# A two-layer diffusion trunk: the slot table written behind the routing and read in the second expert, one modulation bank computed during the routing

## The chip, the core and the metric

The kernel runs on one NeuronCore of a Trainium2 chip. The metric is the device time of one execution in microseconds; the median of three runs stands for the kernel. Engines: PE (TensorE) multiplies matrices, DVE (VectorE) and ACT (ScalarE) do elementwise work, POOL (GpSimd) issues indirect transfers, SP issues most weight loads. The DMA engines move all data; an issuing engine only starts a transfer.

## The reference

Two layers over 256 context and 256 latent tokens of width 1024. Each layer starts from modulation vectors, six per stream, that come from the conditioning alone:

```python
mod_x = split(silu_c @ w_ada + b_ada, 6)        # latents; the same with silu_cc for the context
h  = rms_norm(x, norm1) * (1 + mod[1]) + mod[0]
px = h @ w_in                                   # retention, convolution and latent attention in parallel
x_mid = x + mod[2] * merge_branches(...)
h2 = rms_norm(x_mid, norm2) * (1 + mod[4]) + mod[3]
x  = x_mid + mod[5] * moe(h2)                   # 16 experts in 4 groups, each token goes to 2 experts
```

`moe` scores each token with a shared router, chooses the best group and two experts in it, and adds `gate * (silu(h2 @ w1[e]) * (h2 @ w3[e])) @ w2[e]` over the chosen experts. All is float32. In layer 0 both streams (512 tokens) go through `moe`, in layer 1 the latents only.

## The kernel before

**Precision.** Every float32 weight is split into a high half (`ehi`, a cast on ACT, L1018) and a low half (`elo`, a subtraction on DVE, L1020); a product is three matmuls: high by high and high by low, then low by high (`mm6`, L192 to L195).

**Modulation banks.** `w_ada` of a layer is cut into three banks of 2048 columns. `Ada(l, b)` computes one: eight steps of one 128-row block, each with four matmuls on four column groups of PE (eight in the trace, L274), then a bias add (L278, L281) and four small stores to `modd[l]` (`finish`). `prep` clears and loads the bias rows on POOL (L246 to L256). Bank (0, 0) comes first; the other five, bank (1, 2) last of them, are filled into layer 0's mixing, one step behind each projection (`fill`). Bank (1, 2) holds the vectors 4 and 5 of layer 1, first read far into layer 1. Its blocks come as 1 MB loads into one buffer, `adaw`.

**Routing of layer 0.** Behind the output projection, the logits of four token tiles are computed (L1109); small DVE operations choose the experts (`select`) and number the tokens of each expert (`positions`: two matmuls, L1279 and L1280). An expert takes at most 112 tokens. For experts 0 and 1, `fetch(e, True)` compares slot numbers and finds the token indices with one-hot matmuls (L1591, L1592), casts them (`si`, L1593) and gathers the rows from `h2d` by an indirect transfer on POOL (L1598). For the other experts the indices come from a table: `slot_table` scatters token number and gate of each token's two choices into DRAM (eight indirect transfers, L1568), loads the eight parts back (`tabs`, L1572), adds them up on DVE (L1573) and makes the indices `sis` (L1574).

**Expert loop.** An expert has two projections up (`up`, four quarters each, each quarter one 512 KB piece of `w1` or `w3`), `act`, and the projection down (`finish`, four quarters). In iteration `e` the order is: first `up` of `e`, with the turning of `e - 1`'s hidden rows ahead of its second quarter; down of `e - 1`; second `up` of `e`; `act`; turning of the rows of `e + 1` (`turn_x`, L1609); `fetch(e + 2)`. In iteration 0 the slot table is built behind the first `up`. Weight pieces are loaded in the order of the list `pieces` into 25 buffers; the use of a piece frees its buffer, and `prefetch` then issues the next load on SP. A callable in `later` runs at the next quarter (`follow`).

**Order.** The program's text gives priorities; the framework's scheduler orders each engine's instructions by them and by when it expects an operand, and each engine then runs its instructions strictly in that order. `tc.issue_after(ins)` (`queued`) puts instructions behind another one of their engine.

Of the kernel before, what the change touches and what calls it, by code (L numbers as in the profile page):

```python
# [108 lines left out]
def tile_hybrid(ctx, tc, x, c, ctxt, c_ctx, w_ada, b_ada, norm1, norm2, w_in, ret_decay, ret_gn, w_ret_o,  # L109
# [123 lines left out]
    class Ada:  # L233
# [30 lines left out]
        def step(self, k):  # L264
            l, b = self.l, self.b
            if k == 5:
                self.prep()
            if k == 0:
                self.ps = psa.tile([P, 512], F32, name=nm("psa"), tag="psa")
            if k not in self.w:  # L270
                self.load(k)
            w = self.w.pop(k)
            for g in range(4):
                TE.matmul(self.ps[32 * g:32 * g + 32, :], sC[:, k, :], w[:, g * 512:(g + 1) * 512],  # L274
                          start=(k == 0), stop=(k == KD - 1))
            if k == KD - 1:
                m = self.bias[0]
                V.tensor_tensor(m, self.ps, m, op=ALU.add)  # L278
                if b != 1:
                    q = slice(64, 128) if b == 0 else slice(0, 64)  # L280
                    V.scalar_tensor_tensor(m[q, :], m[q, :], 1.0, self.bias[1][q, :], op0=ALU.add, op1=ALU.mult)  # L281

# [44 lines left out]
    for l in range(DEPTH):  # L327
# [95 lines left out]
        if l == 0:  # L423
# [74 lines left out]
            ma = stA.enter_context(pool(f"mb{l}", side="right"))  # L498
            for al, ab_ in ((0, 1), (0, 2), (1, 0), (1, 1), (1, 2)):
                a = Ada(al, ab_, mx, 1, ps_tile, t2)  # L500
                todo += [(a, k) for k in range(KD + 1)]
# [467 lines left out]
        NA, NB = (7, 6) if l == 0 else (5, 6)  # L969
        pieces = []  # L970
        for e in range(NE):
# [33 lines left out]
        def queued(ins):  # L1005
            return tc.issue_after(ins) if ins is not None else nullcontext()

        def weights(after=(None, None)):

# [12 lines left out]
            prefetch()  # L1022
            return [t.rearrange("p (k n) -> p k n", k=kt) for t in (hi, lo)]


# [81 lines left out]
        def logits_part(t, half):  # L1107
            for k in range(4 * half, 4 * half + 4):
                TE.matmul(lps[0][:, t * NE:(t + 1) * NE], hTs[t, half][:, k % 4 * P:(k % 4 + 1) * P],  # L1109
                          wrs[(T0 + t) // 2][:, k, :], start=(k == 0), stop=(k == KD - 1))  # L1110

# [103 lines left out]
        if l == 0:  # L1215
            offer(3, lambda: wr_.tile([P, 1024], F32, name=nm("wraw"), tag="wraw", bufs=NRAW), REST[l])
            prefetch()
        lps[0] = ps_tile()
        for t in range(NTT):
            ps = ps_tile()  # L1220
            for k in range(KD):
# [7 lines left out]
                if t and k == 5:  # L1229
# [3 lines left out]
                    if t - 1 == 1:  # L1233

                        for tg in ("mr20", "mr40", "mr30"):
                            offer(1, lambda tg=tg: me.tile([P, 1024], F32, name=nm("eraw"), tag=tg), 1000 if tg == "mr30" else REST[l])
                        prefetch()
# [60 lines left out]
        for i in range(4):  # L1298
            offer(1, lambda i=i: zz[:, i, :], FOR[l])
        if l == 0:  # L1300
            offer(ND[l], lambda: et("eraw3", [P, 1024], F32, ND[l]))
            offer(1, lambda: et("fx", [P, 1024]), REST[l])
            prefetch(most=6)
            with queued(h2w[-1]):
                prefetch(nc.gpsimd, 2)
        else:
            offer(1, lambda: me.tile([P, 1024], F32, name=nm("eraw"), tag="mr21"), REST[l])
            prefetch()
# [222 lines left out]
        if l == 0:  # L1531
# [21 lines left out]
            def slot_table():  # L1553
# [19 lines left out]
                V.tensor_reduce(gtab.rearrange("p e v -> p (e v)"), tabs.rearrange("p j n -> p n j"), axis=AX.X, op=ALU.add)  # L1573
                V.tensor_scalar(sis, gtab[:, :, 1], 1.0, 0.0, op0=ALU.subtract, op1=ALU.max)  # L1574

# [8 lines left out]
            def fetch(e, early=False):  # L1584

                if early:
                    si = et("si", [P, 1], I32, 2)
                    ip = ps_tile()
                    for t in range(NTT):
                        oh16 = et("oh16", [P, cap], F16, 4)  # L1590
                        V.tensor_scalar(oh16, C("iota")[:, :cap], posm[:, t, e:e + 1], None, op0=ALU.is_equal)  # L1591
                        TE.matmul(ip[:cap, 0:1], oh16, tok16[:, t:t + 1], start=(t == 0), stop=(t == NTT - 1))  # L1592
                    routed.append(V.tensor_copy(si[:cap, :], ip[:cap, 0:1]).ins)  # L1593
# [59 lines left out]
            def collect(t):  # L1653
# [11 lines left out]
            with tc.issue_after(fetch(1, True)):  # L1665
                prefetch(nc.gpsimd)
            turn_x(0)
            th = None
            for e in range(NE):
# [29 lines left out]
                if e == 0:  # L1699
                    offer(1, lambda: mg.tile([P, 1024], F32, name=nm("eraw"), tag="xe2"), REST[l])  # L1700
# [209 lines left out]
```

## Time and profile before

| | |
|---|---|
| runs | 1657.21 us median (1655.49 to 1659.54) |
| the profiled execution | 1652.17 us, span 1650.4 us |
| mean granted TensorE clock | 0.974 |
| PE, DVE, ACT, POOL busy | 93%, 71%, 51%, 6% of the span |
| moved by DMA | 370.95 MB, mean 225 GB/s |

Times of rows count from the span's start. Layer 0's mixing ends near 552 us, its output projection and routing near 655, its experts near 970; layer 1 follows. A matmul's end is modelled, so the busy share of PE is an upper bound of its use.

### The profile page before, as it was taken

What the parts mean: (1) busy time and instruction counts of PE and PEld (TensorE: products, weight loads), DVE (VectorE), ACT (ScalarE), POOL (GpSimd) and SP (SyncE); (2) the same over time, 40 slices, a digit from 0 to 9 for tenths busy, and PEclk for the clock granted to TensorE, in tenths of its full rate; (3) what the DMA queues carried; (4) which work ended last, traced back from release to release, by engine and by line L of the source; (5) the groups of instructions that cost most, each with busy time, mean ns of one, the idle gap of its engine ahead of it and who ended that gap; (6) DMA issues with size and microseconds to landing.
All of it is one profiled execution on the core that took longest, in us unless ns stands there. A gap on an engine that the chain in (4) does not pass through costs nothing. (4 is left out here: it accounts for less than half of the span.)

```text
span 1650.4 us, 21806 instructions
## 1 busy us (share of the span) xinstructions
PE 1539.1 (93%) x7811; PEld 1191.7 (72%) x7811; DVE 1169.3 (71%) x1996; ACT 842.1 (51%) x1217; POOL 91.4 (6%) x138
## 2 busy tenths in 40 slices
PE   4999999999999996799999978999999989999996
PEld 1577776667767785577777757888877868888775
DVE  2643376436674448789988988668576689999897
ACT  3322233334432323578888854345553457777674
POOL 2010000000010001400001100000000000000000
PEclk9999999999999997999999989999999989999998
DMA  8776354543238357699998946335346569999981
GB/s 321 219 219 217 101 166 150 175 143 113 72 121 305 119 199 237 213 381 387 383 381 311 363 152 188 103 105 151 100 109 199 201 229 356 347 393 331 360 303 66
DMA packets 237129, 370.95 MB, mean 225 GB/s; under 512 B 16018, under 2 KB 133236, under 8 KB 230868
## 3 DMA queue, kind: packets, MB, share of 16 engines
q1 hardware_dynamic: 226464, 344.07, 61.9%
q0 software_dynamic: 6400, 15.13, 2.8%
q10 hardware_dynamic: 4148, 10.27, 1.7%
q8 instruction: 64, 1.05, 0.3%
q14 instruction: 53, 0.43, 0.1%
HBM read 357.69 MB, written 11.73 MB: 224 GB/s over the span
## 5 line engine op out<-in xcount | busy, mean ns | idle before, releaser
L1020 DVE TENSOR_TENSOR elo<-eraw,ehi 128x1024 fp32r<-128x1024 f32 x293 | 346.1, 1219 | 8.3 <-ACT ehi L1018 6.6
L1018 ACT CAST ehi<-eraw 128x1024 fp32r<-128x1024 f32 x293 | 303.3, 1050 | 82.1 <-PE ps L193 45.0
L375 DVE TENSOR_TENSOR wlo<-wraw,whi 128x1024 fp32r<-128x1024 f32 (+1 forms) x146 | 176.3, 1210 | 205.1 <-ACT whi L372 202.9
L372 ACT CAST whi<-wraw 128x1024 fp32r<-128x1024 f32 (+1 forms) x146 | 151.2, 1038 | 287.0 <-PE ps L186 193.9
L185 PE MATMUL ps<-hh,whi 128*128 128x512 f32 (+1 forms) x800 | 287.4, 360 | 1.4 <-ACT hh L418 1.0
L187 PE MATMUL ps<-hh,wlo 128*128 128x512 f32 (+1 forms) x800 | 275.9, 346 | 3.5 <-DVE wlo L375 3.5
L186 PE MATMUL ps<-hl,whi 128*128 128x512 f32 (+1 forms) x800 | 275.4, 345 | 0.2
L185 PEld LDWEIGHTS ps<-hh,whi 128*128 128x128 f32 x800 | 151.4, 189 | 46.1 <-issue 15.8
L187 PEld LDWEIGHTS ps<-hh,wlo 128*128 128x128 f32 x800 | 151.1, 189 | 27.4 <-DVE wlo L375 4.4
L186 PEld LDWEIGHTS ps<-hl,whi 128*128 128x128 f32 x800 | 151.3, 189 | 24.2 <-issue 3.9
L192 PE MATMUL ps<-ehi,xh 128*112 128x512 f32 x256 | 103.0, 402 | 3.7 <-ACT xh L225 3.7
L193 PE MATMUL ps<-ehi,xl 128*112 128x512 f32 x256 | 102.5, 400 | 1.9 <-DVE xl L226 1.9
L192 PE MATMUL ps<-ehi,xgh 128*128 128x512 f32 x256 | 102.3, 400 | 0.2 <-ACT ehi L1018 0.2
L193 PE MATMUL ps<-ehi,xgl 128*128 128x512 f32 x256 | 101.3, 396 | 0.0
L192 PE MATMUL py<-ehi,gg 128*112 128x512 f32 (+1 forms) x240 | 94.6, 395 | 0.1
L193 PE MATMUL py<-ehi,gg 128*112 128x512 f32 (+1 forms) x240 | 93.8, 393 | 0.0
L195 PE MATMUL py<-elo,gg 128*112 128x512 f32 (+1 forms) x240 | 76.0, 398 | 9.1 <-DVE elo L1020 8.4
L1020 DVE TENSOR_TENSOR elo<-raws,ehi 128x1024 fp32r<-128x1024 f32 x68 | 81.1, 1220 | 3.3 <-ACT ehi L1018 2.5
L195 PE MATMUL ps<-elo,xgh 128*128 128x512 f32 x256 | 80.8, 396 | 1.2 <-DVE elo L1020 1.2
L195 PE MATMUL ps<-elo,xh 128*112 128x512 f32 x256 | 80.4, 395 | 0.6 <-DVE elo L1020 0.6
L1018 ACT CAST ehi<-raws 128x1024 fp32r<-128x1024 f32 x68 | 70.5, 1050 | 15.4 <-PE ps L193 10.7
L274 PE MATMUL psa<-adaw,sC 128*32 128x512 f32 x384 | 59.6, 645 | 13.4 <-DMA adaw<-in_w_ada_dram 13.3
(459 smaller groups left out, 2747.9 us busy)
## 6 DMA issues: line engine op xcount, KB each, us to landing
eraw<-in_w_dram SPq DMA_DIRECT2D x293, 512.0 KB
wraw<-in_w_in_dram SPq DMA_DIRECT2D x106, 512.0 KB
adaw<-in_w_ada_dram SPq DMA_DIRECT2D x48, 1024.0 KB
raws<-in_w_dram SPq DMA_DIRECT2D x68, 512.0 KB
wraw<-in_w_dram SPq DMA_DIRECT2D x18, 512.0 KB
wraw<-in_w_out_dram SPq DMA_DIRECT2D x16, 512.0 KB
yd<-ys ACTq DMA_DIRECT2D x16, 448.0 KB
mr<-modd SPq DMA_DIRECT2D x11, 512.0 KB
```

What stands on the lines that cost most here:

```text
L185: TE.matmul(ps, wp[0], xp[0], start=first, stop=False)
L186: TE.matmul(ps, wp[0], xp[1], start=False, stop=False)
L187: TE.matmul(ps, wp[1], xp[0], start=False, stop=last)
L192: TE.matmul(ps, x_[0], w_[0], start=first, stop=False)
L193: TE.matmul(ps, x_[1], w_[0], start=False, stop=False)
L195: ins = TE.matmul(ps, x_[0], w_[1], start=False, stop=last)
L274: TE.matmul(self.ps[32 * g:32 * g + 32, :], sC[:, k, :], w[:, g * 512:(g + 1) * 512], start=(k == 0), stop=(k == KD - 1))
L372: his.append(A.copy(hi[:, :kt * n], raw[:, :kt * n]).ins)
L375: V.tensor_tensor(lo[:, :kt * n], raw[:, :kt * n], hi[:, :kt * n].bitcast(F32), op=ALU.subtract)
L1018: latest["hi"] = A.copy(hi, raw).ins
L1020: latest["lo"] = V.tensor_tensor(lo, raw, hi.bitcast(F32), op=ALU.subtract).ins
```

## The change

Bank (1, 2) is taken out of the mixing. Its blocks become sixteen 512 KB pieces at the head of layer 0's piece list. Four of its steps are issued behind the last logits matmul, four behind the last index matmul of expert 1; its bias add and stores follow in iteration 1. `token_gates` and `slot_table` move from behind the first `up` of expert 0 to in front of it. The reduction of the table, with the fetch for expert 2, becomes `read_table`, which runs behind the second quarter of expert 1's first `up`; the next `elo` is queued behind it. `tabs` and the bias rows use buffers that are needed only later, and `oh32` has two buffers instead of four.

```diff
         def step(self, k):
-            if k == 5:
+            if k == 5 and self.pool is not None:
                 self.prep()
...
             for g in range(4):
-                TE.matmul(self.ps[32 * g:32 * g + 32, :], sC[:, k, :], w[:, g * 512:(g + 1) * 512],
-                          start=(k == 0), stop=(k == KD - 1))
+                wg = w[:, g * 512:(g + 1) * 512] if not isinstance(w, list) else w[g // 2][:, g % 2 * 512:g % 2 * 512 + 512]
+                self.last = TE.matmul(self.ps[32 * g:32 * g + 32, :], sC[:, k, :], wg, start=(k == 0), stop=(k == KD - 1)).ins
+            if k == KD - 1 and self.pool is not None:
+                self.add()
+        def add(self):          # the bias add, as before in step
...
-            for al, ab_ in ((0, 1), (0, 2), (1, 0), (1, 1), (1, 2)):
+            for al, ab_ in ((0, 1), (0, 2), (1, 0), (1, 1)):
...
+            pieces += [(w_ada[1, kk * P:(kk + 1) * P, 4096 + 1024 * h:5120 + 1024 * h], 1) for kk in range(KD) for h in range(2)]
+        n_ada = len(pieces)     # added to the bounds REST and FOR of the buffers
...
+        def raw_piece():
+            i = used[0]
+            used[0] += 1
+            free.append(slot[i])
+            return raws.pop(i)
...
-            if i < 8:
+            if i < n_ada + 8:
                 after = scored[-1], held[0] if held else routed[0]
+            elif len(held) > 1 and held[1] is not None:
+                after, held[1] = (None, held[1]), None
...
+            late_rows = [lambda: et("gg", [P, 8 * cap], F32R, 2)[:, :512].bitcast(F32), lambda: et("late", [P, 512])]
+            late_ada = Ada(1, 2, None, 0, None, lambda: late_rows.pop()())
+            def late_steps(ks, after):
+                with tc.issue_after(after):
+                    for kk in ks:
+                        late_ada.w[kk] = [raw_piece() for _ in range(2)]
+                        late_ada.step(kk)
+                prefetch()
...
-                    oh32 = et("oh32", [P, cap], F32, 4)
+                    oh32 = et("oh32", [P, cap], F32, 2)
...
-                tabs = et("tabs", [CAP, 8, 2 * NE])
+                tabs = et("ohT", [P, L], F32R, 2)[:CAP].bitcast(F32).rearrange("p (j n) -> p j n", j=8)
+                tab.append(tabs)
                 for j in range(8):
                     nc.gpsimd.dma_start(tabs[:, j, :], slotd[j][1:].rearrange("(s e) v -> s (e v)", e=NE))
-                V.tensor_reduce(gtab..., tabs...)
-                V.tensor_scalar(sis, gtab[:, :, 1], 1.0, 0.0, op0=ALU.subtract, op1=ALU.max)
+            def read_table():
+                V.tensor_reduce(gtab..., tab[0]...)
+                si = V.tensor_scalar(sis, gtab[:, :, 1], 1.0, 0.0, op0=ALU.subtract, op1=ALU.max).ins
+                fetch(2)
+                G.memset(gone[0], 0.0)
+                with queued(si):
+                    held.append(V.tensor_copy(gone[1], gone[0]).ins)
...
+            late_steps(range(4), latest["logits"])
             fetch(0, True)
...
             with tc.issue_after(fetch(1, True)):
                 prefetch(nc.gpsimd)
+                late_ada.prep()
+            late_steps(range(4, KD), latest["ip"])
+            with queued(routed[-1]):
+                token_gates()
+                slot_table()
             turn_x(0)
...
                 if e == 0:
                     with queued(routed[-1]):
-                        token_gates()
                         gates(gt[:, :, :NE])
...
-                    with queued(routed[-1]):
-                        slot_table()
...
-                if e + 2 < NE:
+                if e == 0:
+                    later.extend([lambda: None, read_table])
+                elif e + 2 < NE:
                     fetched = fetch(e + 2)
...
+                if e == 1:
+                    late_ada.add()
+                    late_ada.finish()
```

## Rows read from the trace of the kernel before

**Rows 1.** By stage: length, busy us of PE, PEld, DVE, ACT, POOL; clock, DMA, GB/s

```profile
380.00:540.00 160.00, 157.66 (x784) 111.54 (x783) 93.92 (x220) 57.20 (x119) 5.80 (x9) 1.00 0.46 148
640.00:660.00 20.00, 7.33 (x26) 5.58 (x27) 14.93 (x77) 5.68 (x9) 5.47 (x3) 0.50 0.80 277
660.00:680.00 20.00, 19.36 (x100) 14.89 (x100) 16.99 (x52) 13.53 (x16) 10.40 (x10) 0.99 0.67 196
680.00:700.00 20.00, 12.41 (x47) 8.73 (x45) 13.06 (x14) 8.95 (x11) 9.39 (x8) 0.83 0.69 222
760.00:800.00 40.00, 39.52 (x184) 30.04 (x183) 37.21 (x38) 32.55 (x41) 1.83 (x2) 1.00 1.04 392
```

**Rows 2.** Waits of PE, 630 to 720 us: total, times, longest

```profile
PE py L195 <- DVE elo L1020: 7.6, 1, 7.6
PE ps L1609 <- DMA xe<-h2d,si: 6.4, 1, 6.4
PE ps L1279 <- DVE m L1162: 3.4, 1, 3.4
PE ps L1609 <- DMA xe<-h2d,sis: 2.5, 1, 2.5
PE ps L1280 <- DVE sel L1183: 2.3, 1, 2.3
```

**Rows 3.** Timeline around the table: start, duration, instruction, [idle before and releaser]

```profile
677.67 0.62 PE L195 MATMUL ps<-elo,xh 128*112 128x512 f32 x2
...
686.41 0.59 DVE L1573 TENSOR_REDUCE gtab<-tabs 112x32 f32<-112x256 f32 x1 [7.88 <-DMA tabs<-slotd]
...
688.12 3.49 DVE L1020 TENSOR_TENSOR elo<-wraw,ehi 128x1024 fp32r<-128x1024 f32 x3
...
689.00 5.73 POOL L1598 DMA_INDIRECT xe<-h2d,sis  x1 [4.09 <-issue]
```

**Rows 4.** The instructions on `adaw` alone, 380 to 540 us: PE and weight loads

```profile
380.00:540.00 160.00, 8.52 (x64) 1.26 (x64) 1.00 0.46 148
```

**Rows 5.** Timeline at the end of bank (1, 2)

```profile
539.34 0.69 DVE L278 TENSOR_TENSOR t<-psa,t 128x512 f32<-128x512 f32 x1 [6.24 <-PE psa L274]
...
543.01 0.50 PE L187 MATMUL ps<-hh,wlo 128*128 128x512 f32 x1 [2.42 <-DVE wlo L375]
...
543.57 0.40 PE L186 MATMUL ps<-hl,whi 128*128 128x512 f32 x1
...
544.88 0.63 PE L185 MATMUL ps<-hh,whi 128*128 128x512 f32 x1
```

**Rows 6.** Timeline of the first two gathers

```profile
649.14 1.81 POOL L1598 DMA_INDIRECT xe<-h2d,si  x1 [5.81 <-DVE oh L1591]
650.00 0.15 DVE L1593 CAST si<-ps 112x1 int32<-112x1 f32 x1
...
651.26 3.12 POOL L1598 DMA_INDIRECT xe<-h2d,si  x1 [0.30 <-issue]
655.64 1.76 PE L1609 MATMUL ps<-cst,xe 112*128 112x112 f32 x8 [6.39 <-DMA xe<-h2d,si]
```

**Rows 7.** All gathers of L1598: ns min/median/max, first and last start; landing

```profile
L1598 POOL DMA_INDIRECT xe<-h2d,sis x14: 908/921/5728, 689.0 to 925.3; - x14
...
DMA to landing us min/median/max: 6.2/7.8/9.8
```

**Rows 8.** Timeline: issue of four pieces on SP, and their first reading on ACT

```profile
738.85 7.00 SPq L999 DMA_DIRECT2D raws<-in_w_dram  x4
...
777.34 1.06 ACT L1018 CAST ehi<-raws 128x1024 fp32r<-128x1024 f32 x1
```

**Rows 9.** The scatters of L1568: ns min/median/max, first and last start

```profile
L1568 POOL DMA_INDIRECT slotd<-val,ti x8: 963/995/2451, 667.5 to 678.1; - x8
```

**Rows 10.** Timeline of POOL: the preparation of bank (1, 2) in the mixing

```profile
461.16 1.03 POOL L254 DMA_DIRECT2D t<-in_norm_dram  x2
464.04 1.73 POOL L256 TENSOR_SCALAR t<-t 128x512 f32<-128x512 f32 x1 [1.85 <-DMA t<-in_norm_dram]
```

More of the change, by code (lines that the diff above doesn't have):

```diff
@@ L273, in step @@
             for g in range(4):
-                TE.matmul(self.ps[32 * g:32 * g + 32, :], sC[:, k, :], w[:, g * 512:(g + 1) * 512],
-                          start=(k == 0), stop=(k == KD - 1))
[L276 to L281, printed above, removed]
+                wg = w[:, g * 512:(g + 1) * 512] if not isinstance(w, list) else w[g // 2][:, g % 2 * 512:g % 2 * 512 + 512]
[3 more added lines that the diff above has]
+        def add(self):
+            m, b = self.bias[0], self.b
+            V.tensor_tensor(m, self.ps, m, op=ALU.add)
+            if b != 1:
+                q = slice(64, 128) if b == 0 else slice(0, 64)
+                V.scalar_tensor_tensor(m[q, :], m[q, :], 1.0, self.bias[1][q, :], op0=ALU.add, op1=ALU.mult)
         def finish(self):
@@ L970, in tile_hybrid @@
         pieces = []
+        if l == 0:
+            pieces += [(w_ada[1, kk * P:(kk + 1) * P, 4096 + 1024 * h:5120 + 1024 * h], 1) for kk in range(KD) for h in range(2)]
+        n_ada = len(pieces)
         for e in range(NE):
@@ L1108, in logits_part @@
             for k in range(4 * half, 4 * half + 4):
-                TE.matmul(lps[0][:, t * NE:(t + 1) * NE], hTs[t, half][:, k % 4 * P:(k % 4 + 1) * P],
-                          wrs[(T0 + t) // 2][:, k, :], start=(k == 0), stop=(k == KD - 1))
+                latest["logits"] = TE.matmul(lps[0][:, t * NE:(t + 1) * NE], hTs[t, half][:, k % 4 * P:(k % 4 + 1) * P],
+                                             wrs[(T0 + t) // 2][:, k, :], start=(k == 0), stop=(k == KD - 1)).ins
         def logits(t):
@@ L1215, in tile_hybrid @@
         if l == 0:
-            offer(3, lambda: wr_.tile([P, 1024], F32, name=nm("wraw"), tag="wraw", bufs=NRAW), REST[l])
+            offer(3, lambda: wr_.tile([P, 1024], F32, name=nm("wraw"), tag="wraw", bufs=NRAW), REST[l] + n_ada)
             prefetch()
@@ L1235, in tile_hybrid @@
                         for tg in ("mr20", "mr40", "mr30"):
-                            offer(1, lambda tg=tg: me.tile([P, 1024], F32, name=nm("eraw"), tag=tg), 1000 if tg == "mr30" else REST[l])
+                            offer(1, lambda tg=tg: me.tile([P, 1024], F32, name=nm("eraw"), tag=tg), 1000 if tg == "mr30" else REST[l] + n_ada)
                         prefetch()
@@ L1298, in tile_hybrid @@
         for i in range(4):
-            offer(1, lambda i=i: zz[:, i, :], FOR[l])
+            offer(1, lambda i=i: zz[:, i, :], FOR[l] + n_ada)
         if l == 0:
             offer(ND[l], lambda: et("eraw3", [P, 1024], F32, ND[l]))
-            offer(1, lambda: et("fx", [P, 1024]), REST[l])
+            offer(1, lambda: et("fx", [P, 1024]), REST[l] + n_ada)
             prefetch(most=6)
@@ L1306, in tile_hybrid @@
         else:
-            offer(1, lambda: me.tile([P, 1024], F32, name=nm("eraw"), tag="mr21"), REST[l])
+            offer(1, lambda: me.tile([P, 1024], F32, name=nm("eraw"), tag="mr21"), REST[l] + n_ada)
             prefetch()
@@ L1569, in slot_table @@
                                                      out_offset=bass.IndirectOffsetOnAxis(ap=ti[:, i, t:t + 1], axis=0))
-                tabs = et("tabs", [CAP, 8, 2 * NE])
+                tabs = et("ohT", [P, L], F32R, 2)[:CAP].bitcast(F32).rearrange("p (j n) -> p j n", j=8)
+                tab.append(tabs)
                 for j in range(8):
                     nc.gpsimd.dma_start(tabs[:, j, :], slotd[j][1:].rearrange("(s e) v -> s (e v)", e=NE))
-                V.tensor_reduce(gtab.rearrange("p e v -> p (e v)"), tabs.rearrange("p j n -> p n j"), axis=AX.X, op=ALU.add)
-                V.tensor_scalar(sis, gtab[:, :, 1], 1.0, 0.0, op0=ALU.subtract, op1=ALU.max)
+            tab = []
+            def read_table():
+                V.tensor_reduce(gtab.rearrange("p e v -> p (e v)"), tab[0].rearrange("p j n -> p n j"), axis=AX.X, op=ALU.add)
+                si = V.tensor_scalar(sis, gtab[:, :, 1], 1.0, 0.0, op0=ALU.subtract, op1=ALU.max).ins
[3 more added lines that the diff above has]
+                    held.append(V.tensor_copy(gone[1], gone[0]).ins)
             def gate(e):
@@ L1591, in fetch @@
                         V.tensor_scalar(oh16, C("iota")[:, :cap], posm[:, t, e:e + 1], None, op0=ALU.is_equal)
-                        TE.matmul(ip[:cap, 0:1], oh16, tok16[:, t:t + 1], start=(t == 0), stop=(t == NTT - 1))
+                        latest["ip"] = TE.matmul(ip[:cap, 0:1], oh16, tok16[:, t:t + 1], start=(t == 0), stop=(t == NTT - 1)).ins
                     routed.append(V.tensor_copy(si[:cap, :], ip[:cap, 0:1]).ins)
@@ L1699, in tile_hybrid @@
                 if e == 0:
-                    offer(1, lambda: mg.tile([P, 1024], F32, name=nm("eraw"), tag="xe2"), REST[l])
+                    offer(1, lambda: mg.tile([P, 1024], F32, name=nm("eraw"), tag="xe2"), REST[l] + n_ada)
                     prefetch()
-                if e + 2 < NE:
+                if e == 0:
+                    later.extend([lambda: None, read_table])
+                elif e + 2 < NE:
                     fetched = fetch(e + 2)
```

1 line of the change is left out of this document (added).

## The prediction

> **What bounds the kernel now.** The page says that TensorE (PE) is busy 93% of the span, so I look for the stretches where it is not. The table by stage [rows 1] gives them. In 380 to 540 us, the second half of layer 0's mixing, PE is busy 157.66 of 160 us: that stretch is PE's, and work taken from it is time. In 640 to 660 us PE has 7.33 of 20 us at a granted clock of 0.50, its lower level (1.2 GHz): the routing, a chain of small VectorE (DVE) operations. In 680 to 700 it has 12.41; from 760 on 39.52 of 40, with DVE at 37.21 and a DMA share of 1.04. So the expert loop is PE's again, with DVE and the DMA engines close behind.
>
> PE's own waits around the routing [rows 2] name the holes: 3.4 and 2.3 us for DVE operations of the routing and 6.4 for the first expert's rows; later 7.6 us for a low half `elo`, and 2.5 us for the third expert's rows. The timeline [rows 3] shows behind what that `elo` stood: DVE read the slot table (L1573) at 686.41 after 7.88 us of waiting for `tabs`, and the next elos came after it. PE had used up its finished low halves and stood. Only then could the third expert's rows be fetched (689.00).
>
> **The change, part by part.** *The bank leaves the mixing.* Its 64 matmuls take 8.52 us in 380 to 540 [rows 4], 1.07 for each of eight steps, all on a busy PE: minus 8.5. They were also cover for softmax waits. PE idled only 2.3 of 160 us [rows 1]; I give back 1.0 (between 0 and 2.3). At the bank's end DVE does its bias add L278 (0.69 us) and a second operation as long ahead of the `wlo` for which PE waits 2.42 us; and a little later PE is at the lower clock, 0.63 us a matmul against 0.40 [rows 5]. Without the two operations the wait is about 1.1 shorter (they overlap their neighbours a little). Eight matmuls at the lower clock cost about 1.8; a wait of 1.3 may or may not bring them on, so I take half. Mixing: -8.5 + 1.0 - 1.1 - 0.9 = -9.5, between -12.5 and -6.
>
> *The bank enters the routing.* Four steps go behind the last logits matmul, four behind the second expert's index matmuls. PE's waits there leave 3.4 + 2.3 and then 6.4 us [rows 2]. Four steps are 4.3 us at the upper clock and 8.5 at the lower one (twice the row). At 0.50 they would overrun by 2.8 and 2.1; I take 0, since steady matmuls went with a risen clock after the old start (0.99 in 660 to 680 [rows 1]). PE then also starts the first expert at the upper clock: about 4 us at half speed become 2, so -1.9. Against that, sixteen buffers are refilled while the first rows are gathered. That gather released PE 6.5 us after its issue [rows 6]; the fourteen later ones take 6.2 to 9.8, median 7.8 [rows 7]: +1.3. Together -0.6, between -2 and +6. The bias add, 1.4 us in two operations, moves into the second expert, where DVE has 7% free: +0.6 (0 to 1.4). Its four stores go out on a POOL that idles there: 0.
>
> *The loads.* The sixteen pieces of the bank stand at the head of the piece list and take the buffers in which expert weights waited. At 392 GB/s [rows 1] one piece of 512 KB takes 1.34 us, sixteen take 21.4. Cover: in the steady loop four pieces issued from 738.85 are first read at 777.34 [rows 8], 38 us later, and none of PE's waits [rows 2] names a weight load. A queue with such a lead swallows sixteen pieces: 0, bounded by 21.4.
>
> *The slot table.* It costs before: 7.6 for the wait, 2.5 for the third expert's rows, and some 1.6 for about 3 us of matmuls at the lower clock behind the wait (the mean is 0.83 over 680 to 700 [rows 1]): 11.7. From the first scatter (667.5 [rows 9]) to the reduction (686.41 [rows 3]) it took 18.9 us. When can the first scatter start now? Its inputs need about twenty small DVE operations, like the index cast of 0.15 us or a little longer, behind that cast (650.00 [rows 6]): 654. POOL is in the second gather until 654.4 [rows 6]. Behind that gather also stands the bank's preparation: two memsets (I put them at 1.0 together), six small loads (3.1; two of them took 1.03) and a scaling of 1.73 that waits for loads [rows 10]. If POOL does memsets and loads first and the scaling in between, the scatters run as if from 660.2, and the table stands at 679.2. `read_table` comes behind the second quarter of the second expert's first projection, and the third quarter's `elo` is held behind it: reduction, index and elo end about 2.0 us later, at 681.2. PE wanted that elo at 677.67 [rows 3]; now about 1.6 earlier (0.6 from above, 1.0 because the table's small operations no longer stand among the elos): 676.1. So PE still waits 5.1 us, and the lower clock behind it costs 1.6 again. The third expert's rows then have ten quarters of 1.4 us before they are needed, more than the 9.8 of the slowest gather: the 2.5 goes. Table: 5.1 + 1.6 - 11.7 = -5.0. Bounds: POOL takes the scatters first, table at 673.3, no wait: -11.7. The whole preparation first, with the scaling's wait of 1.85 and slow loads: table at 683.4, -0.8.
>
> One rule speaks against this part. From 688.12 DVE ran elos back to back, and the gather issued at 689.00 held POOL 5.73 us [rows 3], where the median one takes 0.92 [rows 7]. The Trainium skill ("SBUF — State Buffer", section "Who interferes with whom") says that a VectorE instruction with two SBUF inputs contends with a GpSimd instruction that reads SBUF, and that the loser blocks fully; that gather agrees. The eight scatters mostly do not, though elos ran among them too: 0.96 to 2.45 us, median 1.0 [rows 9]. I keep the scatters at their rows; the other case is a rival.
>
> *Two `oh32` buffers instead of four:* the third and fourth comparison wait for matmuls, for two experts: +0.6 (0 to 3).
>
> Sum: -9.5 - 0.6 + 0.6 + 0 - 5.0 + 0.6 = -13.9. The profiled execution took 1652.17 (span 1650.4): 1638.3. It lies 5.0 below the median of the runs, 1657.21; from there 1643.3.
>
> **The rivals.** (1) The forecast: 1643, its own range 1637 to 1648. (2) The table is read without a wait: another 6.7 off, 1636.6. For it: POOL idles between the second gather and the old first scatter, 13 us; against it: the preparation in front. (3) Port contention: every scatter waits out one elo of 1.2 us, the table comes 9.8 later, 1653. That is the rule named above; one gather shows it, one scatter in eight perhaps. (4) The bank was cover in the mixing, and other waits appear when it goes: the mixing gives 3, not 9.5: 1650. For it: PE waits there already come from DVE; against it: a PE idle of 1.5%. (5) The other sign: the weights come late. The full 21.4 us show, and 1643.3 + 21.4 = 1664.7, slower than before. It decides once the lead between landing and first use falls to nothing. For it: DMA at 1.04 has little left to catch up with. Against it: a lead of 38 us, larger than the debt. (6) The bank's matmuls run at the lower clock and push the routing by 4.9, with a slow gather on top: 1650.
>
> **How the numbers follow.** Chances: (1) 0.48, (2) 0.15, (3) 0.13, (4) 0.12, (5) 0.07, (6) 0.05. A measurement of this kernel tells about 0.3% (5 us) from no change. Faster than 1652.2: (1), (2), (6), nearly all of (4) and a third of (3), less a rest: 0.81. Slower than 1662.2: (5) and a rest: 0.08. Within: 0.11. The range 1633 to 1655 takes in (1) to (4) and (6) and leaves out (5) and the far end of (2).
>
> **What would show it.** No `adaw` rows of this bank between 380 and 540 us, and that stretch shorter by 8 to 12 us. The bank's 64 matmuls between 630 and 655 instead, and a granted clock near 1.0 when the first expert starts. The first scatter 4 to 12 us behind the second index cast, the reduction's wait shorter than 7.88 us, a PE wait of 0 to 9 us behind it, and none for the third expert's rows. Waits for weight loads in the first three experts would mean (5); scatters of 2 us and more, (3). I am wrong above all if POOL's order or pace brings the table later than it came before, or if the mixing does not shorten.

## The result, and the profile after

The changed kernel took 1636.11 us in the median of four runs (1633.98 to 1638.47), the kernel before 1658.38 beside it (1655.49 to 1660.18): ratio 0.9868, interval 0.9841 to 0.9896. The forecast was 1643, with a range of 1633 to 1655. A later set of six runs, beside eleven of the kernel before, gave 1641.24 against 1654.85, 0.9902 (0.9875 to 0.993). So the gain is 14 to 22 us by medians, which move that much from set to set. (A ratio here and below compares all runs of a set, and can differ by up to 0.002 from the quotient of the medians.) The profiled execution took 1638.47 us (span 1636.7) against 1652.17: 13.7 less, where the prediction's sum was 13.9. Two things hide in that agreement. In the trace of the changed kernel the start (up to 335.07 us, before 331.35), which the change does not touch, is 3.7 us longer; and the terms are off in both directions. The stages show it.

By stage, changed kernel (length, PE busy with its instructions, granted clock, DMA share, GB/s); the first row is layer 0 from the 41st cast `whi` to the first store of `h2d`:

```profile
335.07:609.11 274.04, 270.13 (x1288) 1.00 0.40 131
380.00:540.00 160.00, 157.83 (x761) 1.00 0.37 112
620.00:640.00 20.00, 14.79 (x81) 0.75 0.84 313
640.00:660.00 20.00, 16.48 (x78) 0.82 1.05 379
660.00:680.00 20.00, 13.93 (x69) 0.83 1.04 369
680.00:700.00 20.00, 19.76 (x93) 1.00 0.69 232
```

The first of these for the kernel before:

```profile
331.35:619.76 288.41, 281.32 (x1352) 0.99 0.47 154
```

The mixing takes 14.4 us less: PE has 64 matmuls fewer and is busy 11.2 us less, and stands 3.2 us less. Behind it, PE is busy 16.48 of the 20 us from 640 to 660, at a clock of 0.82 instead of 0.50; 680 to 700, where before had a hole [rows 1], is whole, but 660 to 680 now has one. These stretches do not hold equal work, since the routing now starts 10.7 us earlier (609.11 instead of 619.76); the table of the experiments compares equal work.

PE's waits of the changed kernel, 610 to 740 us (total, times, longest):

```profile
PE ps L1572 <- DVE oh L1571: 5.8, 1, 5.8
PE ps L1645 <- DMA xe<-h2d,si: 3.0, 1, 3.0
PE ps L1306 <- DVE sel L1209: 2.3, 1, 2.3
```

Against [rows 2]: the waits for `elo` and for the third expert's rows are gone, that for the first rows (L1645) is halved, since PE works on the bank meanwhile. New is a wait of 5.8 us for a one-hot, the fourth comparison into `oh32` of `slot_gates(1)`. No wait for a weight load is among them.

The timeline around the table, changed kernel (start, length, idle before it and its releaser):

```profile
642.60 1.75 POOL L1634 DMA_INDIRECT xe<-h2d,si  x1 [0.18 <-DVE oge L1341]
644.34 0.55 POOL L246 MEMSET late<- 128x512 f32 x1
...
645.27 2.11 POOL L249 DMA_DIRECT2D late<-in_b_ada_dram  x4
...
649.49 1.03 POOL L1594 DMA_INDIRECT slotd<-val,ti  x1 [1.10 <-DMA xe<-h2d,si]
...
655.48 1.53 POOL L256 TENSOR_SCALAR gg<-gg 128x512 f32<-128x512 f32 x1
...
661.15 1.81 POOL L1594 DMA_INDIRECT slotd<-val,ti  x1 [0.31 <-issue]
...
667.72 0.52 POOL L1599 DMA_DIRECT2D ohT<-slotd  x1 [0.99 <-DMA slotd<-val,ti]
...
673.00 0.58 DVE L1604 TENSOR_REDUCE gtab<-ohT 112x32 f32<-112x256 f32 x1 [6.15 <-DMA ohT<-slotd]
673.49 0.27 DVE L1571 TENSOR_SCALAR oh<-cmoe,posm 128x112 f32<-128x112 f32 x1
...
673.82 0.56 PE L1572 MATMUL ps<-gt,oh 128*112 128x17 f32 x2 [5.83 <-DVE oh L1571]
...
674.64 1.26 POOL L1634 DMA_INDIRECT xe<-h2d,sis  x1 [5.14 <-PE ps L1384]
...
675.25 0.62 DVE L1393 SCALAR_TENSOR_TENSOR gg<-ps,gg 128x448 fp32r<-128x448 f32 x1
675.79 3.49 DVE L1035 TENSOR_TENSOR elo<-eraw,ehi 128x1024 fp32r<-128x1024 f32 x3
```

POOL does memsets, loads, then scatters, with the scaling (L256) between the fourth and the fifth, as the prediction took it; the first scatter comes 8.2 us behind the second index cast (641.32), inside the 4 to 12 forecast. DVE stands in front of the reduction from 666.85; the one-hot is behind it in DVE's order, and PE behind the one-hot.

### The profile page after: what moved, and what is told of

It reads as the page before. It is cut to its first block, busy times and chain, and to the rows that moved or that the text cites. A ratio compares the mean times of both kernels' runs of the same rounds, so it can differ in the third digit from the quotient of the medians.

```text
span 1636.7 us, 21817 instructions
## 1 busy us (share of the span) xinstructions
PE 1538.8 (94%) x7811; PEld 1192.1 (73%) x7811; DVE 1168.9 (71%) x1997; ACT 842.3 (51%) x1217; POOL 84.9 (5%) x139
## 5 line engine op out<-in xcount | busy, mean ns | idle before, releaser
L1035 DVE TENSOR_TENSOR elo<-raws,ehi 128x1024 fp32r<-128x1024 f32 x72 | 86.2, 1223 | 4.3 <-ACT ehi L1033 3.8
L1033 ACT CAST ehi<-raws 128x1024 fp32r<-128x1024 f32 x72 | 74.8, 1050 | 19.3 <-PE ps L193 12.6
L275 PE MATMUL psa<-adaw,sC 128*32 128x512 f32 x320 | 52.7, 673 | 13.2 <-DMA adaw<-in_w_ada_dram 13.1
```

What stands on the lines that cost most here:

```text
L275: self.last = TE.matmul(self.ps[32 * g:32 * g + 32, :], sC[:, k, :], wg, start=(k == 0), stop=(k == KD - 1)).ins
L1035: latest["lo"] = V.tensor_tensor(lo, raw, hi.bitcast(F32), op=ALU.subtract).ins
```

## The experiments

Each run was profiled, and the table reads all traces at the same four marks: A, the 41st cast `whi` (before: 331.35); B, the first store of `h2d` in layer 0's routing; C, the first transposes of the fourth expert's rows; D, the first `rf` on ACT near the end. The three last columns are the lengths of A to B (mixing), B to C (routing and three experts) and C to D, less 288.41, 101.18 and 923.21 of before. Two traces of one kernel (after and e12, e7 and e13) differ by up to 0.8 in a column, so smaller differences are not read. The expectations say "the first row of layer 1's h2" for B; the store in layer 0's routing is meant.

| run | A | B | C | D | mixing | routing, experts | rest |
|---|---|---|---|---|---|---|---|
| before | 331.35 | 619.76 | 720.94 | 1644.15 | | | |
| after | 335.07 | 609.11 | 709.59 | 1630.85 | -14.4 | -0.7 | -2.0 |
| e12, after again | 334.34 | 609.05 | 708.70 | 1629.66 | -13.7 | -1.5 | -2.3 |
| e1, bank only | 334.94 | 610.11 | 714.14 | 1636.03 | -13.2 | +2.9 | -1.3 |
| e2, table only | 333.62 | 621.59 | 719.78 | 1641.01 | -0.4 | -3.0 | -2.0 |
| e3, bank left out | 332.04 | 606.55 | 708.56 | 1634.11 | -13.9 | +0.8 | +2.3 |
| e4, `oh32` 3 | 333.68 | 608.39 | 709.36 | 1630.34 | -13.7 | -0.2 | -2.2 |
| e5, `cum` later | 335.17 | 610.45 | 712.32 | 1634.14 | -13.1 | +0.7 | -1.4 |
| e6, preparation first | 332.55 | 609.50 | 706.80 | 1628.48 | -11.5 | -3.9 | -1.5 |
| e10, e6 and `oh32` 3 | 335.32 | 609.83 | 704.14 | 1625.10 | -13.9 | -6.9 | -2.3 |
| e7, e10 and `cum` | 332.72 | 606.89 | 699.41 | 1624.67 | -14.2 | -8.7 | +2.1 |
| e13, e7 again | 333.03 | 606.91 | 699.76 | 1624.68 | -14.5 | -8.3 | +1.7 |
| e8, e2 and a gap | 334.16 | 622.46 | 718.05 | 1642.17 | -0.1 | -5.6 | +0.9 |
| e11, read later | 333.01 | 607.89 | 706.96 | 1631.50 | -13.5 | -2.1 | +1.3 |

The last column goes with the clock. In the runs e7, e13, e3 and e11 (+1.3 to +2.3) a stretch of about 6.8 us at the lower clock stands in layer 1 near 1240 us, e8 and the kernel before (+0.9 and 0) have half of that, the others (-2.3 to -1.3) none. The edits lie ahead of C, so the column is not read for what they do. Still it may belong to a kernel: both traces of e7's kernel have the stretch, and neither of the changed kernel's has it. No run here separates the two.

**The two halves apart.** e1 is the changed kernel with the table's old place, and its reduction and `sis` inside `slot_table` again:

```diff
-            with queued(routed[-1]):
-                token_gates()
-                slot_table()
...
+                    with queued(routed[-1]):
+                        slot_table()
...
-                if e == 0:
-                    later.extend([lambda: None, read_table])
-                elif e + 2 < NE:
+                if e + 2 < NE:
```

> The changed kernel with the slot table put back behind the first expert's first projection and read there; only the bank is moved. Theory (the terms add up: mixing 14.4, routing and gather give back about 4, slot table 4.4): about 9 to 11 us under the kernel before in the medians, ratio 0.9935 to 0.9945; the mixing is as short as in the changed kernel (274 us from 331 to the first row of layer 1's h2), the index si of the first expert comes 2.0 us later behind that row than in the kernel before, and the old holes in 680 to 700 us are back: a PE wait of 5 to 8 us for an elo behind a table reduction that waits more than 5 us, and one of 1 to 3 us for the third expert's rows. Rival A (the bank's matmuls cost nothing in the routing and the table gave nearly nothing): 18 us or more under before, ratio 0.989 or less. Rival B (the mixing's gain is not the bank's but run variation): ratio 0.997 or more, mixing longer than 284 us.

Measured: 1641.84 against 1657.17, 0.9916 (0.9884 to 0.9949). The medians lie 15.3 us apart, more than the 9 to 11 expected; from A to C the traces differ by 10.4, which fits. Mixing and the `elo` hole (5.1) came as expected; a wait for the third expert's rows did not come back, though their gather took 6.88 us on POOL. `si` came only 0.2 us late behind B (28.75 us against 28.59), not 2.0, and yet the stage cost 2.9. PE's first transposes stand 10.8 us behind the issue of the first gather, against 6.5 [rows 6]: that is where the bank costs, and part of it disappeared in the table's hole behind it. Rival B is out, with a mixing of 275.2 us. Rival A (0.989 or less) is not out by the times, whose interval takes it in; it falls by the traces, +2.9 in the routing here and -3.0 for the table alone in e2.

e2 has the bank back in the mixing:

```diff
...
-            for al, ab_ in ((0, 1), (0, 2), (1, 0), (1, 1)):
+            for al, ab_ in ((0, 1), (0, 2), (1, 0), (1, 1), (1, 2)):
...
-            late_steps(range(4), latest["logits"])
...
-                late_ada.prep()
-            late_steps(range(4, KD), latest["ip"])
...
```

> The changed kernel with the bank put back into layer 0's mixing; only the slot table and its reading are moved, with two oh32 buffers. Theory: the old waits for the low half and for the third expert's rows are gone; the scatters start behind the second gather without the bank's loads and memsets in front of them, 4 to 6 us earlier than in the changed kernel, so the table's reduction waits 0 to 2 us, and PE's wait at the second expert's one-hot matmuls shrinks from 5.8 to under 2. Then 6 to 11 us under before, ratio 0.9935 to 0.9965. Rival (the wait of 5.8 comes from the two oh32 buffers whatever the table does): the wait stays over 4 us and the time is within 5 us of before, ratio 0.997 or more.

Measured: 1650.04 against 1657.17, 0.9969 (0.995 to 0.9988). The one-hot's wait is gone and that for `elo` is 1.6, so the rival falls by its wait; its time, 0.997 or more, is not told apart from this one. Two parts of the expectation fall too. The first scatter came no sooner behind `si` (10.0 us; changed kernel 9.8): its index `ti` stands in DVE's order behind `xl` (L226), the low half of the first expert's rows, for which DVE stood idle for 3.22 us, until 658.59. And a wait of 5.2 for the third expert's rows ate most of the gain. The trace of e2 shows why, POOL and then DVE:

```profile
680.47 11.47 POOL L1634 DMA_INDIRECT xe<-h2d,sis  x1 [5.18 <-issue]
```

```profile
679.66 3.49 DVE L1035 TENSOR_TENSOR elo<-eraw,ehi 128x1024 fp32r<-128x1024 f32 x3
683.06 3.49 DVE L1035 TENSOR_TENSOR elo<-wraw,ehi 128x1024 fp32r<-128x1024 f32 x3
686.47 3.49 DVE L1035 TENSOR_TENSOR elo<-eraw,ehi 128x1024 fp32r<-128x1024 f32 x3
689.88 1.22 DVE L1035 TENSOR_TENSOR elo<-raws,ehi 128x1024 fp32r<-128x1024 f32 x1
691.01 0.68 DVE L1374 SCALAR_TENSOR_TENSOR eth<-eth,ps 112x512 f32<-112x512 f32 x1
```

The gather's issue holds POOL to 691.94, as long as ten elos run with nothing between them.

**The gap.** e8 is e2, with the elos waiting until that issue is over (the part that differs from e2):

```diff
-                fetch(2)
-                G.memset(gone[0], 0.0)
+                with tc.issue_after(fetch(2)):
+                    G.memset(gone[0], 0.0)
```

> The run with the table alone, and the held elo now waits until GpSimd has issued the third expert's gather (the small clearing of gone stands behind the gather on GpSimd, instead of ahead of it). Theory (the gather is shut out by the elos that run back to back): the gather lasts 1 to 2 us instead of 11.47, PE's wait of 5.2 for the third expert's rows goes, the held elo comes 1 to 2 us later, and the end is 3 to 5 us under the run with the table alone. Rival (the gather is slow for another reason, such as the load on the DMA queues): it lasts 5 us and more all the same and the wait stays.

The gather in e8:

```profile
683.77 0.97 POOL L1634 DMA_INDIRECT xe<-h2d,sis  x1 [4.80 <-issue]
```

The wait for the rows is gone, that for `elo` is 3.3. From the second expert's first transposes to C, e8 takes 42.60 us (675.45 to 718.05), e2 48.01 (671.77 to 719.78): 5.4 less. From B to C it is 2.6 less, because in e8 those transposes stand 2.8 us later behind B, ahead of the place of the edit. The medians are 1645.14 against 1661.66, 0.9916 (0.9889 to 0.9942). The gather's length is settled: it is the elos.

**The mixing alone.** e3 is the kernel before without the bank's product:

```diff
         def step(self, k):
             l, b = self.l, self.b
+            if (l, b) == (1, 2):
+                return
```

> The kernel before with the loads, matmuls and bias sum of layer 1's third bank left out (its bias alone is stored as the vectors), nowhere made up for. This prices the removal by itself. Theory (matmuls 8.5, the wait of 2.4 at the bank's end and the lower clock behind it): the mixing is 13 to 15 us shorter and so is the run, ratio 0.990 to 0.9925; PE's busy time in the mixing falls by 10 to 12 and its idle time by 2 to 4. Rival A (the prediction's own term): 9.5 us, ratio 0.9943, the wait for wlo still there at about 1.3. Rival B (the missing 21 us of loads is worth something too, because SP's queue or the DMA engines held later loads): more than 17 us, ratio 0.9895 or less, with further gain behind the mixing.

Measured: 1642.84 against 1657.17, 0.9928 (0.9907 to 0.9949), and in the trace of e3:

```profile
332.04:606.55 274.51, 270.15 (x1288) 1.00 0.41 131
```

PE is busy 11.2 less and idle 2.7 less, 13.9 in sum. PE's longest waits from 380 to 550 us, the kernel before and then e3:

```profile
PE ps L187 <- DVE wlo L375: 2.4, 1, 2.4
```

```profile
PE ps L915 <- DVE pe L901: 1.4, 2, 1.0
```

The wait for `wlo` is gone, as the theory has it. Rival B falls by the time. Rival A's 0.9943 lies inside the interval, so it falls by the trace, where the mixing gives 13.9 and not 9.5, and no wait of 1.3 is left.

**What holds the one-hot.** e4:

```diff
-                    oh32 = et("oh32", [P, cap], F32, 2)
+                    oh32 = et("oh32", [P, cap], F32, 3)
```

> The changed kernel with three oh32 buffers in place of two. Theory (the fourth one-hot of the second expert stands behind the table's reduction only because its buffer came free too late; two buffers set the wait of 5.8 us): the one-hots are all written ahead of the reduction, PE's wait there falls under 1 us, and PE runs on until the elo held behind the index, for which it then waits 0 to 4 us: 1 to 5 us under the changed kernel, ratio to before 0.984 to 0.986. Rival (the table's lateness sets it; the wait only moves from the one-hot to the held elo): the same 5 to 6 us of PE wait stand at the first matmul of the third quarter, and the time is that of the changed kernel, ratio 0.9868 within 0.002.

Measured: 1639.77 against 1657.17, 0.9911 (0.9877 to 0.9944), not faster than the changed kernel (0.9868 and 0.9902). The rival holds. PE runs past the one-hot and stands some 2 us of work later, for the elo that is held, and longer than the 5 to 6 expected:

```profile
675.28 1.19 PE L195 MATMUL ps<-elo,xh 128*112 128x512 f32 x2 [7.42 <-DVE elo L1035]
```

**What makes the table late.** e6 moves the preparation ahead of the first gather:

```diff
+            with tc.issue_after(h2w[-1]):
+                late_ada.prep()
...
                 prefetch(nc.gpsimd)
-                late_ada.prep()
```

> The changed kernel with the bank's preparation on GpSimd (two memsets, six small loads, one scaling) issued behind the last store of h2 instead of behind the second gather. Theory (the preparation stands in front of the scatters, as the prediction put it): first scatter 2 to 3 us earlier, no scaling among the scatters (1.5 us), so the table's reduction 4 to 5 us earlier behind si than the 33.3 us of the changed kernel, PE's wait of 5.8 down to 1 to 2, the end 3 to 4 us under the changed kernel. Rival, from the run with the table alone (no preparation at all, yet its first scatter came 8.4 us behind si, as in the changed kernel, because VectorE's index operations stand behind turn_x and the first rows): only the scaling goes, 1.5 us, and the end is within 2 us of the changed kernel.

Measured: 1636.31 against 1661.66, 0.9861 (0.9823 to 0.9899). The table stands 29.4 us behind `si` instead of 33.3, 3.9 earlier where 4 to 5 were expected, and the first scatter 7.7 instead of 9.8. From B to C it is 3.2 us less than in the changed kernel's first trace, 2.4 less than in its second (e12). But PE's wait is 4.7, not 1 to 2: it is the one-hot's again. e10 takes the third buffer as well:

> The changed kernel with the preparation moved and three oh32 buffers, the clearing of cum left as it was. Theory (two waits stand behind each other, the fourth one-hot behind the table's reduction and the held elo behind the index; three buffers alone won nothing because the table was late, the early table alone little because the one-hot waited): PE's wait at the second expert falls from 4.7 to under 1.5 us and the third expert's rows come in time, 4 to 6 us gained over the run with the preparation alone between the first row of h2 and the third expert, and as fast as the run with all three. Rival (the clearing of cum made the difference): PE's wait stays at 3 us or more, and the gain over the run with the preparation alone is under 2 us.

Measured: 1633.14 against 1654.85, 0.9857 (0.9829 to 0.9884). Its waits at the second expert:

```profile
PE ps L1572 <- DVE oh L1571: 1.0, 1, 1.0
```

From B to C e10 takes 3.0 us less than e6, with the table 29.0 us behind `si`. The wait goes as the theory said. The gain is smaller than the 4 to 6 expected: the wait itself gives 3.7 (4.7 to 1.0), and the first transposes stand 0.5 us later behind B than in e6, behind a `si` that came 2.0 later (30.71 against 28.75).

**The bank's steps in the routing.** e5 puts two memsets of layer 1 behind the last elo of layer 0 that the text has issued by then. In the changed kernel they stand on DVE until PE's L1305 has read `cum`, and L1305 stands behind the first 32 matmuls of the bank. PE and then DVE of the changed kernel (the row names no releaser for the idle 2.43 us, but the memset starts 0.2 to 0.3 us behind the end of L1305 here, in e12, e1, e6 and the kernel before, and in e5 DVE does not stand idle there):

```profile
627.05 1.89 PE L1135 MATMUL ps<-wrs,t 128*128 128x16 f32 x8 [0.68 <-ACT t L1129]
628.87 5.96 PE L275 MATMUL psa<-eraw,sC 128*32 128x512 f32 x32
634.76 0.43 PE L1305 MATMUL ps<-cum,cst 128*128 128x64 f32 x2
```

```profile
632.66 0.17 DVE L1193 TENSOR_TENSOR e<-e,cmoe 128x16 f32<-128x16 f32 x1
635.26 0.20 DVE L1175 SCALAR_TENSOR_TENSOR gs<-gs,m,cmoe 128x4 f32<-128x4 f32 x1 [2.43 <-issue]
635.27 0.07 DVE L1153 MEMSET cum<- 128x16 f32 x1
```

```diff
+        before_ = latest if l else {}
...
-        V.memset(cum[:, 0, :], 0.0)
-        V.memset(cumg[:, 0, :], 0.0)
+        with queued(before_.get("lo")):
+            V.memset(cum[:, 0, :], 0.0)
+            V.memset(cumg[:, 0, :], 0.0)
```

> The changed kernel with layer 1's two small clearing operations on cum and cumg queued behind the routing, so that VectorE no longer stands 2.43 us for PE's ones-times-cum product that itself stands behind the bank's first four steps. Theory (the bank's steps cost the routing 2.0 us through this one VectorE wait): the index si of the first expert comes 2.0 us sooner behind the first row of layer 1's h2 than in the changed kernel, as soon as in the kernel before (28.6 us against 30.6); of the 2.0 the end keeps little, because PE then waits for the table instead (PE's wait at the second expert rises from 5.8 by what is won unless the table moves with it): 0 to 2 us in the end. Rival (the bank's matmuls themselves are in the way, at the lower clock): si comes no sooner than 30 us behind that row.

Measured: 1641.78 against 1661.66, 0.9893 (0.9855 to 0.9931). `si` came 27.8 us behind B instead of 30.6, so the rival falls. But the first gather came 3.0 us behind `si` instead of 0.4 and the table 37.0 behind it: PE's wait rose to 7.2, and from B to C e5 takes 1.4 us more than the changed kernel's first trace. The DMA records show what the gather stood for. It reads `h2d`, and the packets of the last row store end 28.1 us behind B in the kernel before, 29.1 in the changed kernel and 29.3 in e5. In ten of the fourteen traces the gather starts 1.3 to 1.5 us behind those packets, and 0.6 to 2.8 behind the end of the index cast; in the other four (after, e4, e10, e11) it starts 0.3 behind the end of the cast. By these traces it waits for the later of the two, and an index at 27.8 wins nothing over one at 29. The first scatter stands 9.0 to 9.4 us behind that gather in the changed kernel's traces and in e5. e12 shows that the memsets are only part:

> The changed kernel once more, beside the others on the same chip. Ratio to before 0.984 to 0.990. Between the first row of h2 and the third expert it should lose and win the same as before (0.7 us won against the kernel before) if its first four bank steps run at the lower clock again, and 2 us more won if the lower clock ends earlier there, as in the runs with the bank alone and with the preparation moved.

Measured: 1641.24 against 1654.85, 0.9902, just outside the 0.984 to 0.990. The same kernel's `si` came 29.1 behind B this time, and from B to C e12 won 0.8 us more than the first trace, where 2 had been expected. In e12:

```profile
627.00 1.06 PE L1135 MATMUL ps<-wrs,t 128*128 128x16 f32 x8 [0.68 <-ACT t L1129]
628.00 5.34 PE L275 MATMUL psa<-eraw,sC 128*32 128x512 f32 x32
```

The clock was at its lower level from 628.8 to 632.3 us, in the first trace of after from 626.8 to 633.6, over the last logits matmuls (L1135) and most of the bank's 32; of the 1.4 us between the two traces the logits have 0.8 and the bank's matmuls 0.6. Where the lower clock lasted 3.4 us there and the memsets are as in the changed kernel (e1, e6, e12), `si` came 28.75 to 29.13 us behind B, where it lasted 6.8 (after, e4, e10, e11) 30.5 to 30.8. In e5, e7 and e13 it lasted 3.4 too, and with the memsets moved `si` came at 27.8, 28.6 and 28.6, so that the memsets are worth about 1 us at most there.

**Read later.** e11 has the third buffer and one more empty place ahead of `read_table`:

```diff
-                    oh32 = et("oh32", [P, cap], F32, 2)
+                    oh32 = et("oh32", [P, cap], F32, 3)
...
-                    later.extend([lambda: None, read_table])
+                    later.extend([lambda: None, lambda: None, read_table])
```

> The changed kernel with three oh32 buffers and the table read one quarter of a projection (about 2 us of PE work) later; the preparation stays ahead of the scatters, so the table comes as late as in the changed kernel. Theory (a hole in PE is the table's arrival less the place where it is read): PE's wait falls from 7.4 (three buffers) to 5 or 5.5, and 2 us are gained over the run with three buffers; the third expert's rows still come in time, unless the elos run back to back and hold the gather, in which case a wait of some us for the rows eats the gain. Rival (the reading holds PE's elo wherever it stands, since the elos queue behind it): the wait stays at 7 and nothing is gained.

Measured: 1639.07 against 1654.85, 0.989 (0.9864 to 0.9916). PE's wait is 3.9 instead of 7.4, less than the 5 to 5.5 expected, and 1.9 us are won from B to C against e4, as expected. The gather lasted 6.94 us beside six elos in a row, but the rows still came in time.

**A version that beats both.** e7 joins e4, e5 and e6; e13 is e7 once more.

> The changed kernel with three oh32 buffers, the clearing of cum moved, and the preparation moved: the three together. Theory: the sum of the parts, 3 to 6 us under the changed kernel, ratio to before 0.982 to 0.9855. Rival (the third expert's gather: in the run with the table alone GpSimd's gather lasted 11.47 us, exactly as long as the run of back-to-back elos on VectorE behind the index, against 1.26 in the changed kernel where a gap came after 1.2 us): once the table is early, the elos run back to back and shut the gather out; a wait of 3 to 6 us for the third expert's rows takes the place of the one removed, and the end is within 2 us of the changed kernel.

> The three edits together once more, beside the changed kernel on the same chip. Theory: 5 to 8 us under the changed kernel, ratio to before 0.980 to 0.985. Rival (the part that layer 1 gave back in its first profile, 3.1 us, belongs to it): 2 to 4 us under.

Measured: 1632.61 against 1661.66, 0.9846 (0.9804 to 0.9887); again 1633.04 beside 1641.24 of the changed kernel and 1654.85 of the kernel before, 0.9857 (0.9828 to 0.9885), a median 8.2 us below the changed kernel. e10, without e5's edit, ran in the same set at 1633.14, so the times show nothing for that edit; from B to C e7 takes 1.8 less than e10, and its last column loses more than that. e13's rival is right that the part lost in layer 1 comes again (+1.7 in the table's last column, against -2.3 in e12), but not that only 2 to 4 us are left: 8.2 by the medians, 5.0 between the two profiled executions. PE's waits at one-hot and elo are 0.3 and 0.2 in e7. That is rival 2, the table read without a wait: 8.0 us less from B to C than in the changed kernel's first trace (e10: 6.2) and 7.1 less than in its second, where it had been priced at 6.7. The feared wait for the third expert's rows does not come: the operation L1395 (`gg`), with one input in PSUM, falls between the first elo and the run of elos, and the gather took 1.27 us.

## Why the prediction came out right, and where its steps did not

**The mixing, -9.5 (bounds -12.5 to -6): -14.4, and -13.1 to -14.5 in all but one of the other kernels without the bank there** (e6, -11.5, is the only one with a stretch at the lower clock inside the mixing, 368.9 to 372.3 us). The matmuls were worth their row [rows 4]. The steps that failed are "about 1.1 shorter" for the `wlo` wait, half of the lower clock behind it, and the 1.0 given back. [Rows 5] say more than was read from them: DVE stood 6.24 us at L278 for PE's last bank matmul, with `wlo` behind it. What goes is not only the length of two operations, but the wait of DVE in front of them. e3 shows the sizes: the whole wait of 2.42 goes, the lower clock behind it (544.5 to 548.0 before) goes, no other wait takes their place (the waits at softmax, 1.2 and 1.0 before, are 0.8 and 1.4). Rival 4 is out. Some 1.0 us of PE's busy time that went is not accounted for.

**The bank in the routing, -0.6 (bounds -2 to +6): +3.8 up to the first expert's transposes.** The 0 taken for the overrun of the steps failed: in the changed kernel the first 32 matmuls took 5.96 us, mostly at the lower clock, and `si` came 2.0 us later behind B. This is rival 6's mechanism at a part of its price, and it varies from run to run. Since the gather also waits for the last row store, it started 1.6 us later, and in e12, with `si` only 0.5 later, still 1.1 later. The gather's +1.3 was too small: the first transposes stand 8.6 us behind its issue (8.0 to 10.8 in the nine other runs with the bank there, 5.9 to 6.9 in the four without it). From its issue to these transposes, before and then the changed kernel (length, PE busy, clock, DMA share, GB/s):

```profile
649.14:655.64 6.50, 0.12 (x1) 0.50 0.69 200
640.12:648.76 8.64, 5.64 (x35) 0.79 1.04 384
```

The refill of the buffers that the prediction named is there; that it makes the rows late is argued from this, and no run takes it away alone. The prediction's range for the later gathers was misread, too: of the landings in [rows 7] the slowest, 9.8, is the second gather's, and the ten recorded ones of the later gathers are 6.2 to 8.7, with the median as stated. The upper clock was forecast at the first expert; it was at the lower one from 650.7 to 654.1, yet not for as long as before (636.7 to 660.6).

**The loads, 0:** right. No wait for a weight load, so rival 5 is out. The bias add's +0.6 was not measured by itself.

**The slot table, -5.0 (bounds -11.7 to -0.8): -4.0,** from the second expert's first transposes (11.1 less than before counted from A) to C (15.1 less). POOL's order was as taken. The table took longer than forecast: 23.5 us from the first scatter to the reduction, where 18.9 and the scaling (1.73) had been counted; the other 2.9 are not accounted for. PE's wait was 5.8 instead of 5.1, and behind the one-hot instead of the elo; e4 shows that the elo would have had it.

**`oh32`, +0.6:** 0 while the table is late (e4), 3.0 once it is early (e6 against e10). These are two waits in series: the price of the missing buffer appears when the wait for the table goes.

**Rival 3 by halves.** The changed kernel's scatters took 0.97 to 1.81 us, so they did not each wait out an elo. The gather does: 5.73 before [rows 3], 6.88 in e1, 11.47 in e2, 6.94 in e11, each about as long as a run of 6 to 10 elos without a gap, and 0.97 in e8, where they wait. In the changed kernel, where `gg`, an operation with one input in PSUM, came behind the first elo, it took 1.26. The Trainium skill ("SBUF — State Buffer", section "Who interferes with whom") lets a VectorE instruction with two SBUF inputs contend with a GpSimd instruction that reads SBUF, and one with at most one SBUF input, outside the 2-port modes, not; these gathers agree, with 5.73 to 11.47 us beside elos alone and 1.26 where `gg` came. The section has the shared ports held for a whole instruction; here the block outlasted ten. Whether a long gather costs PE a wait is another matter: 2.5 us before, 5.2 in e2 (0 in e8, without the elos beside it), but 0 in e1 and e11, with 6.88 and 6.94. Why these two did not wait stays open.

**The sum.** -14.4 in the mixing and -0.7 from B to C make 15.1 of gain, where the steps made 9.5 + 4.4 = 13.9: a mixing 4.9 better than forecast paid for a routing 3.7 worse. That the total came out right is luck: two errors of opposite sign, the first of them outside its own bounds. The median does not tell the rivals apart either: 1636.1 is nearly rival 2's 1636.6, though PE stood 5.8 us for the table. The halves add up: e1 and e2 together give -13.6 - 0.1.

## What to carry to other kernels

When a block of work leaves a stage, read not only its own operations but which engine stands waiting for it in its order: the wait in brackets belongs to the price. When a read is held for a late result, the hole is the result's arrival less the place of the read; take away what delays the arrival first (here the preparation), and then the buffers that make the next wait. From B to C the buffers alone won nothing, the early table alone 3.2 us, both 6.2. An early index is worth little if the transfer that it starts cannot be issued: look whether the data that it reads are stored by then, and leave a gap between the VectorE operations beside it.

## What was not expected of the hardware

A gather's issue on GpSimd lasted from 0.97 to 11.47 us for the same 112 rows, by what VectorE ran beside it, while the changed kernel's scatters, with single elos among them, stayed at 0.97 to 1.81. And in two executions of the same kernel `si` stood 1.4 us apart behind B, by where a stretch of lower clock lay over the logits and the bank's first 32 matmuls.
